# Two normalised copies of the residual stream exchange their buffers, and one is split ahead of the other

## The chip, the cores and the metric

The kernel runs on one core of one Trainium2 chip. The metric is the device time of one execution in microseconds (us); lower is better. Four engines matter here: TensorE (PE, matrix products into PSUM), VectorE (DVE), ScalarE (ACT), and SyncE (SP), whose queue issues most of the loads. Each engine works through its own list of instructions, and engines wait for one another by semaphores.

## The reference

The reference is a two-layer decoder trunk over 512 tokens of width 1024 in float32, held here with features on the 128 partitions, so that the stream `x` is eight tiles `x[0]` to `x[7]` of 128 x 512. Layer 0 mixes with a gated DeltaNet, layer 1 with sliding-window attention whose keys and values come from the stream as it stands after layer 0; each layer also attends to 256 memory tokens and ends with a SwiGLU network. What bears on this change is this:

```
x = x + swiglu(rms_norm(x, ln_ffn[layer]), w_gate_up[layer], w_down[layer])
if layer == N_A_LAYERS - 1:
    kv = rms_norm(x, ln_kv) @ w_kv          # keys and values of layer 1
...
h = rms_norm(x, ln_mix[layer])              # next layer
proj = h @ swa_w_q[bl]                      # its queries, and the memory queries
```

So once layer 0 is done, the same `x` is normalised twice with two gains: with `ln_mix[1]` for the queries, and with `ln_kv` for keys and values.

## The kernel before

**Arithmetic.** Products are made in a reduced form of float32. Each operand is split into a high and a low part, `hi = round(g*x)` by a copy on ACT (line 138) and `lo = g*x - hi` on DVE (line 154 with a gain, line 151 without), and each product is three matmuls: `wh*ah`, `wh*al`, `wl*ah` (`mm3`, lines 196 to 202). In a trace the activations' parts are called `h` and `l`, those of a weight tile `whi` and `wlo`. The row's scale of the norm, `rstd`, is not applied to `x` but to each product afterwards, so a split needs the finished `x[k]` and a gain, and nothing else. `pair` (line 160) takes a high and a low tile of 128 x 512 from a pool.

**The pools.** Two pools hold such pairs, eight each: `apool` and `bpool`. A slot can be written again when its last reader has run. Around the end of layer 0 they are used so:

| data | pool before | read until |
|---|---|---|
| normalised input of layer 0's SwiGLU | `bpool` | the last gate and up columns of layer 0 |
| SwiGLU products of layer 0's last third, six pairs (`whole`, line 1182) | `apool` | the last row of layer 0's down projection |
| layer 1's input with `ln_mix[1]` (list `h` of `swa`) | `apool` | the last of the queries |
| layer 1's input with `ln_kv` (list `hk`) | `bpool` | keys and values |
| outputs of layer 1's attentions (`beside`, line 1587) | `bpool` | layer 1's output projection |
| normalised input of layer 1's SwiGLU (`output`) | `apool` | layer 1's gate and up columns |
| products of layer 1's SwiGLU (`ffn8`) | `bpool` | its down projection |

**The stages around the change.** Layer 0's SwiGLU ends with eight rows of its down projection (lines 1273 to 1282). Each row `m` is 18 matmuls over the six pairs of products; then DVE scales the product (`fu<-pj,rstd`), adds it to `x[m]` (`x<-fu,x`), and ACT squares `x[m]` for the next norm's sum (`sq`, summed on DVE as `sqa`). The next stage is `swa` (line 1526). It fetches two memory tiles, splits `h` (line 1535), and begins the queries: tile 7 and tile 6 are the memory queries. `queries(6)` runs its 24 matmuls over `h[0]` to `h[7]`, then two steps (6 matmuls) of `queries(7)`, and then forms `rstd` of the new stream (`rstd_from`, line 1454): the summed squares are split (`rs`), multiplied by ones in two matmuls (`pt<-rs,ones`), and turned into `rstd` by a Ln and an Exp on ACT; DVE multiplies the rotary tables by it (`cosT`, `sinT`) and scales the product of tile 6 (`q<-pj,rstd`). In the text `hk` is split after `queries(6)` (line 1616). Then follow the rest of `queries(7)`, `score(6)` (`qk<-mk,q`), the keys (the first reader of `hk`), the values, `score(7)`, and the six pairs of windowed heads, whose queries, scores, softmax and output rows are interleaved.

**What sets the order.** The tile library lays out each engine's list when the program is built: it takes instructions that are ready by its own reckoning, the earlier in the program text the sooner, and an instruction whose slot is not free by that reckoning is passed over for one that can go. `nosync(a, b)` (line 114) adds an edge that places `a` behind `b` in that layout and costs no wait on the chip. Loads of weights are issued on SP's queue when one of the two `wraw` buffers comes free.

Of the kernel before, what the change touches and what calls it, by code (L numbers as in the profile page):

```python
# [39 lines left out]
G_MIX, G_FFN, G_KV, G_FIN = (0, 8), (16, 24), 32, 40  # L40
# [44 lines left out]
class Builder:  # L85
# [25 lines left out]
    def bank(self, tag, shape=(P, T)):  # L111
        return self.t(self.pp, list(shape), F32, tag, self.pbufs[tag])
# [131 lines left out]
    def build(self):  # L244
        tc, nc, a = self.tc, self.nc, self.a
        with ExitStack() as st:
            opened = lambda name, **kw: tc.tile_pool(name=name, bufs=1, reuse_waits="tile", **kw)
            pool = lambda name, **kw: st.enter_context(opened(name, **kw))
            cp = pool("const")
            self.wpool, self.apool = pool("w"), pool("acta")  # L250
            self.dpool = pool("scratch", space=DRAM)
            self.load_constants(cp)
            self.weng = nc.vector
            with opened("layer0", side="right") as self.mpool:
                with self.banks(pj=3, g=2, sc=3):
                    with opened("early", side="right") as ep:
                        self.mem_and_norm(ep)
                    with opened("gdn", side="right") as gp:
                        mix = self.gdn(gp)
                    self.bpool, xp = pool("actb"), pool("x")  # L260
                    self.x = [self.t(xp, [P, T], F32, f"x{k}") for k in range(KD)]
                    for k in range(KD):
                        nc.sync.dma_start(self.x[k], a["xT"][:, k, :])
                    self.rstd, self.cosT, self.sinT = (self.t(xp, [P, T], F32, n) for n in ("rstd", "cosT", "sinT"))
                    h = self.output(xp, 0, mix)
            with opened("ffn0", side="right") as fp, self.banks(pj=2, g=6):
                self.ffn8(fp, xp, 0, h, self.apool, rope=True)
            with self.banks(pj=2, qk=2, pt=2), opened("swa", side="right") as sp:
                h = self.output(xp, 1, *self.swa(sp))
            with opened("ffn1", side="right") as fp, self.banks(pj=2, g=6):  # L270
                self.ffn8(fp, xp, 1, h, self.bpool)

    def load_constants(self, cp):
        nc, a = self.nc, self.a
# [791 lines left out]
    def output(self, xp, layer, mix, begun=()):  # L1066

        nc, a = self.nc, self.a
        self.weng = nc.vector
        h = []  # L1070
        self.acc = None
        hpool = self.apool if layer else self.bpool
        bank = lambda m: self.bank(("pj", "pj", "pt")[m % 3] if begun else "g" if m % 4 == 3 else "pj")
        n, ws, lows = len(begun), [], []

        def early(m):
            if begun and n <= m < KD:
                ws.append(self.weight(a["wout"][layer, m]))
                lows.append(self.low)

        done = [list(row)[-1] for row in begun]
        for i in range(2):
            early(n + i)
        for m in range(KD):
            ps = done[m] if m < n else list(
                self.row(layer, m, mix, lambda: bank(m), ws.pop(0) if ws else None))[-1]
            self.ended = self.tt(nc.vector, self.x[m], ps, self.x[m], ALU.add)
            if m >= n - 1:
                early(m + 3)
            hl = self.pair(hpool)  # L1090
            self.split_gain(self.x[m], self.gain(G_FFN[layer], m), *hl)
            if m == 0 and lows:
                self.nosync(self.low, lows[-1])
            h.append(hl)
            self.acc = self.accumulate(xp, self.acc, self.x[m], m)
        self.behind = self.loaded if layer else None
        return h
# [428 lines left out]
    def swa(self, sp):  # L1526
        nc, a = self.nc, self.a
        memK, memV = self.fetch(sp, "mk"), self.fetch(sp, "mv")
        hk, h, qs, mix = [], [], {}, {}
        def normed(t, base, pool):  # L1530
            for k in range(KD):
                t.append(self.pair(pool))
                self.split_gain(self.x[k], self.gain(base, k), *t[k])

        normed(h, G_MIX[1], self.apool)
        sinks = self.small[:, 12:24].rearrange("p (b t) -> p t b", b=2)
        kk, vv = [], []

        def behind(step):

            return self.scalings[step - 1] if step > 0 else None

        def queries(t):
            w = self.weight(a["wq"][t], after=behind(t - 2) if t < 6 else None)
            ps = self.bank("pj")
            for k in range(KD):
                self.mm3(ps, w, k, h[k], k == 0, k == KD - 1)
                yield
            if t == 6:
                list(zip(range(2), beside7))  # L1550
                self.rstd_from(self.acc, *(self.t(sp, [P, T], F32R, "rs", 2) for _ in range(2)), after=self.last)
                for table in (self.cosT, self.sinT):
                    self.tt(nc.vector, table, table, self.rstd, ALU.mult)
            qs[t] = self.t(sp, [P, T], F32, "q", 3)
            if t < 6:
                self.rope(sp, ps, qs[t])
            else:
                self.tt(nc.vector, qs[t], ps, self.rstd, ALU.mult)
# [25 lines left out]

        def beside(t, *works):

            out = self.pair(self.bpool)
            steps = self.weighed(sp, got[t], *((vv, t) if t < 6 else (memV, t - 6)), out, t < 6)
            for work in works:
                list(work)  # L1590
                next(steps, None)
            mix[t] = out
            return self.ready, out
# [9 lines left out]
        def half():  # L1603
            if not free:
# [6 lines left out]
                         after=lambda m=m: behind(min(m + 4, 7)), **(own if m > 2 else {})) for m in range(5)]  # L1611
        some = lambda work, n: (next(work) for _ in range(n))
        got = {}
        beside7 = queries(7)
        list(queries(6))
        normed(hk, G_KV, self.bpool)
        list(beside7)
        score(6)
        keys()
# [7 lines left out]
        for t in range(6):  # L1627
            score(t)
            work, n = (queries(t + 2), (2, 3, 4)) if t < 4 else (rows[t - 4], (1, 1, 2))
            o = beside((6, 7, 0, 1, 2, 3)[t], *(some(work, i) if i < 4 else work for i in n))  # L1630
            softmax((7, 0, 1, 2, 3, 4)[t])
            settle(*o)
        o = beside(4, some(rows[0], 2), some(rows[1], 2), some(rows[2], 3))
        softmax(5)
        settle(*o)
        for m, n in ((2, 3), (3, 4)):
            list(some(rows[m], n))
        settle(*beside(5, some(rows[3], 2), some(rows[4], 3), (next(rows[m]) for m in (4, 4, 4, 0, 1))))
        for m in range(2, 5):
            list(some(rows[m], 1))  # L1640
# [110 lines left out]
```

## Time and profile before

| | |
|---|---|
| median of 3 runs | 1113.31 us (1112.72 to 1115.05) |
| time of the profiled execution | 1112.83 us |
| its span, first to last instruction | 1111.1 us |
| mean granted TensorE clock | 0.998 |
| busy: PE, PE weight loads, DVE, ACT | 99%, 90%, 84%, 63% of the span |

A row of the timeline gives the start, the time, the engine, the line, the operation, what it writes and reads, the shape, and how many instructions are merged into the row; brackets give idle time ahead of it and what ended it. Successive matmuls overlap in the trace, and so the distance from one start to the next tells how fast PE goes through them, not the duration of one. Layer 0's down rows stand from about 593 to 627 us from the start of the span, the start of `swa` from 627 us on.

### The profile page before, as it was taken

To read this page: it belongs to the slowest core of one execution; us is meant where nothing else is said; L and a number is where in the kernel's file an instruction comes from. 1 tells how busy PE (TensorE), PEld (TensorE's weight loads), DVE (VectorE), ACT (ScalarE), POOL (GpSimd) and SP (SyncE) were. 2 spreads that over 40 slices of the span, in tenths; PEclk is the share of its full clock that TensorE was granted. 3 is DMA by queue.
4 is the path that set the end of the run, shared out by engine and by line. 5 is a ranking of instruction groups with operands and counts; after the bars stand their busy time and mean duration, and the time that the engine had idled before them with its cause. 6 is when DMAs were issued, how large, how long until landed. Compare 5 with 4: busy or idle time off the path is not lost.

```text
span 1111.1 us, 21262 instructions
## 1 busy us (share of the span) xinstructions
PE 1100.6 (99%) x7957; PEld 998.9 (90%) x7957; DVE 937.0 (84%) x1890; ACT 697.2 (63%) x1470; POOL 105.9 (10%) x129
## 2 busy tenths in 40 slices
PE   9999999999999999999999999999999999999997
PEld 8888778877899999999998777788899999999996
DVE  7685977667899999999997977839999999998964
ACT  7588674466566656665565654866667466655644
POOL 0000000000011121112110000000111111121101
PEclk9999999999999999999999999999999999999999
DMA  8244352234567787778753321114677776778632
GB/s 320 98 151 142 114 142 82 90 98 145 150 173 183 189 190 191 179 184 199 191 147 99 117 74 40 58 58 142 159 176 192 189 195 184 186 198 203 148 86 90
DMA packets 81146, 165.36 MB, mean 149 GB/s; under 512 B 18588, under 2 KB 20148, under 8 KB 81044
## 3 DMA queue, kind: packets, MB, share of 16 engines
q1 hardware_dynamic: 64436, 133.87, 38.0%
q0 software_dynamic: 16320, 29.89, 16.5%
q8 instruction: 62, 1.02, 0.4%
q14 instruction: 40, 0.33, 0.1%
q10 hardware_dynamic: 288, 0.26, 0.1%
HBM read 156.98 MB, written 7.01 MB: 148 GB/s over the span
## 4 chain that ended last, share of the span: by engine, by line
PE 92%; DVE 5%; ACT 1%; issue 1%; DMA 0%; SPq 0%; DVEq 0%; ACTq 0%
PE g L144 54%; PE pj L144 26%; PE sc L144 6%; PE qk L144 3%; PE pt L144 2%; PE pt L148 1%; DVE wlo L151 1%; PE g L148 1%; DVE l L154 1%; DVE big L151 1%; DVE x L151 1%; DMA early<-in_early 0%; DVE fu L151 0%; DVE qv L154 0%; DVE btmp L151 0%
## 5 line engine op out<-in xcount | busy, mean ns | idle before, releaser
L138 ACT ACTIVATE whi<-wraw 128x512 fp32r<-128x512 f32 (+2 forms) x357 | 250.6, 711 | 161.4 <-PE g L144 66.3
L151 DVE TENSOR_TENSOR wlo<-wraw,whi 128x512 fp32r<-128x512 f32 (+2 forms) x357 | 280.5, 793 | 36.8 <-ACT whi L138 31.8
L144 PE MATMUL g<-T,whi 128*128 128x256 f32 x1280 | 228.3, 279 | 0.0
L144 PE MATMUL g<-h,wlo 128*128 128x256 f32 (+1 forms) x780 | 222.7, 285 | 0.6 <-DVE wlo L151 0.6
L144 PE MATMUL g<-l,whi 128*128 128x256 f32 (+1 forms) x780 | 222.6, 285 | 0.0
L144 PE MATMUL g<-h,whi 128*128 128x256 f32 (+1 forms) x780 | 222.4, 285 | 0.0
L144 PEld LDWEIGHTS g<-T,whi 128*128 128x128 f32 x1280 | 194.9, 188 | 0.5 <-DVE fu L154 0.5
L144 PE MATMUL pj<-h,whi 128*128 128x512 f32 (+1 forms) x460 | 182.0, 398 | 0.0
L144 PE MATMUL pj<-l,whi 128*128 128x512 f32 (+1 forms) x460 | 180.4, 393 | 0.4 <-DVE l L154 0.3
L144 PE MATMUL pj<-h,wlo 128*128 128x512 f32 (+1 forms) x460 | 179.8, 391 | 0.0
L144 PE MATMUL g<-T,wlo 128*128 128x256 f32 x640 | 178.5, 279 | 0.0
L144 PEld LDWEIGHTS g<-h,wlo 128*128 128x128 f32 x780 | 146.6, 188 | 2.8 <-DVE wlo L151 1.1
L144 PEld LDWEIGHTS g<-l,whi 128*128 128x128 f32 x780 | 146.6, 188 | 1.9
L144 PEld LDWEIGHTS g<-h,whi 128*128 128x128 f32 x780 | 146.6, 188 | 1.8
L144 PEld LDWEIGHTS g<-T,wlo 128*128 128x128 f32 x640 | 120.3, 188 | 0.0
L144 PEld LDWEIGHTS pj<-h,whi 128*128 128x128 f32 x460 | 86.4, 188 | 20.7 <-issue 4.1
L144 PEld LDWEIGHTS pj<-h,wlo 128*128 128x128 f32 x460 | 86.5, 188 | 18.0 <-issue 0.9
L144 PEld LDWEIGHTS pj<-l,whi 128*128 128x128 f32 x460 | 86.5, 188 | 17.8 <-DVE l L154 1.2
L138 ACT ACTIVATE whi<-ws 128x512 fp32r<-128x512 f32 x112 | 70.1, 626 | 38.9 <-PE g L144 36.8
L151 DVE TENSOR_TENSOR wlo<-ws,whi 128x512 fp32r<-128x512 f32 x112 | 77.1, 689 | 2.9 <-ACT whi L138 2.9
L1394 POOL DMA_DIRECT2D ws<-in_wgu x40 | 35.1, 878 | 414.6 <-DVE l L154 203.9
L138 ACT ACTIVATE fs<-g 128x256 f32<-128x256 f32 x168 | 61.5, 366 | 1.1 <-PE g L144 0.7
(398 smaller groups left out, 1929.6 us busy)
## 6 DMA issues: line engine op xcount, KB each, us to landing
wraw<-in_wgu SPq DMA_DIRECT2D x48, 512.0 KB, 4.0
ws<-in_wgu SPq DMA_DIRECT2D x80, 256.0 KB, 3.6
ws<-in_wgu POOLq DMA_DIRECT2D x80, 256.0 KB, 4.9
wraw<-in_win SPq DMA_DIRECT2D x26, 512.0 KB, 4.0
wraw<-in_wgu SPq DMA_DIRECT2D x40, 256.0 KB, 5.4
wraw<-in_wout SPq DMA_DIRECT2D x16, 512.0 KB, 3.4
ws<-in_wdn SPq DMA_DIRECT2D x32, 256.0 KB, 5.7
wraw<-in_wdn SPq DMA_DIRECT2D x16, 512.0 KB, 3.8
```

What stands on the lines that cost most here:

```text
L138: self.copied = self.nc.scalar.activation(out, in_, AF.Copy, **kw).ins
L144: return self.nc.tensor.matmul(out, lhsT, rhs, start=start, stop=stop, skip_group_check=more).ins
L148: return self.nc.tensor.transpose(out, in_, self.ident[:k, :k]).ins
L151: return eng.tensor_tensor(out=out, in0=a, in1=b, op=op).ins
L154: return self.nc.vector.scalar_tensor_tensor(out=out, in0=in0, scalar=scalar, in1=in1, op0=op0, op1=op1).ins
L1394: nc.gpsimd.dma_start(s1, a22, accum_op=ALU.add)
```

## The change

`h` and `hk` exchange their pools, and everything in layer 1 that follows in their slots exchanges with them, so that each pool still holds eight pairs at most: `h` goes into `bpool` and after it the normalised input of layer 1's SwiGLU; `hk` goes into `apool`, after it the attentions' outputs and the products of layer 1's SwiGLU. With that, `output` takes its pairs from `bpool` in both layers. New besides: `normed` can take two instructions as `after`, and each split of `hk` (its copy on ACT and its subtraction on DVE) is ordered behind the last split of `h` on the same engine by `nosync`. No instruction is added or removed.

```diff
@@ build
-                self.ffn8(fp, xp, 1, h, self.bpool)
+                self.ffn8(fp, xp, 1, h, self.apool)
@@ output
-        hpool = self.apool if layer else self.bpool
...
-            hl = self.pair(hpool)
+            hl = self.pair(self.bpool)
@@ swa
-        def normed(t, base, pool):
+        def normed(t, base, pool, after=()):
             for k in range(KD):
                 t.append(self.pair(pool))
                 self.split_gain(self.x[k], self.gain(base, k), *t[k])
-
-        normed(h, G_MIX[1], self.apool)
+                for ins, other in zip((self.copied, self.low), after):
+                    self.nosync(ins, other)
+
+        normed(h, G_MIX[1], self.bpool)
+        made = self.copied, self.low
@@ beside
-            out = self.pair(self.bpool)
+            out = self.pair(self.apool)
@@ swa, after queries(6)
-        normed(hk, G_KV, self.bpool)
+        normed(hk, G_KV, self.apool, made)
```

## The prediction

> **What bounds the kernel now.** I read the page first: the busy shares (of a span of 1111.1 us), and the engines on the chain that ended last.
>
> ```profile
> PE 1100.6 (99%) x7957; PEld 998.9 (90%) x7957; DVE 937.0 (84%) x1890; ACT 697.2 (63%) x1470; POOL 105.9 (10%) x129
> PE 92%; DVE 5%; ACT 1%; issue 1%; DMA 0%; SPq 0%; DVEq 0%; ACTq 0%
> ```
>
> PE carries 92% of the chain, so the change is worth what it alters in PE's waiting. The edit changes no instruction, only when the two sets of splits run; the place to look is therefore the seam from layer 0's last down row to the first queries. Next I read PE's timeline there and counted starts.
>
> ```profile
> 622.96 0.39 PE L144 MATMUL pj<-h,whi 128*128 128x512 f32 x1
> ...
> 627.04 0.39 PE L144 MATMUL pj<-h,whi 128*128 128x512 f32 x1
> ...
> 630.44 0.39 PE L144 MATMUL pj<-h,whi 128*128 128x512 f32 x1
> 630.92 0.50 PE L144 MATMUL pj<-l,whi 128*128 128x512 f32 x1
> ...
> 632.19 0.39 PE L144 MATMUL pj<-h,whi 128*128 128x512 f32 x1
> 632.85 0.50 PE L144 MATMUL pj<-l,whi 128*128 128x512 f32 x1 [0.27 <-DVE l L154]
> ...
> 634.81 0.62 PE L144 MATMUL pt<-rs,ones 128*128 128x512 f32 x2
> ...
> 639.49 2.00 PE L144 MATMUL qk<-mk,q 64*128 64x256 f32 x16
> 641.41 0.50 PE L144 MATMUL pj<-h,whi 128*128 128x512 f32 x1
> ```
>
> The last down row is the 18 matmuls from 622.96 to 627.04, so undisturbed PE takes 4.08/18 = 0.227 us for each. From 627.04 the 24 matmuls of queries(6) and 6 of queries(7) run until the sum of squares at 634.81: 7.77 us for 30, where 30 x 0.227 = 6.80 would do. **0.97 us is lost**, visibly at two starts that come 0.48 and 0.66 us after the one before: the low parts of h[5] (630.92) and of h[7] (632.85). The second bracket names the releaser: DVE's line 154. Then I read what DVE and ACT did there.
>
> ```profile
> 628.86 0.75 DVE L154 SCALAR_TENSOR_TENSOR l<-x,gains,h 128x512 fp32r<-128x512 f32 x1
> 629.52 0.69 DVE L151 TENSOR_TENSOR x<-fu,x 128x512 f32<-128x512 f32 x1
> 630.12 1.41 DVE L154 SCALAR_TENSOR_TENSOR l<-x,gains,h 128x512 fp32r<-128x512 f32 x2
> 631.44 0.69 DVE L151 TENSOR_TENSOR sqa<-sqa,sq 128x512 f32<-128x512 f32 x1
> 632.04 1.42 DVE L154 SCALAR_TENSOR_TENSOR l<-x,gains,h 128x512 fp32r<-128x512 f32 x2
> 633.37 0.69 DVE L151 TENSOR_TENSOR rs<-sqa,rs 128x512 fp32r<-128x512 f32 x1
> 633.97 0.75 DVE L154 SCALAR_TENSOR_TENSOR l<-x,gains,h 128x512 fp32r<-128x512 f32 x1
> 634.63 2.37 DVE L151 TENSOR_TENSOR wlo<-wraw,whi 128x1024 fp32r<-128x1024 f32 x2
> 636.92 0.69 DVE L151 TENSOR_TENSOR cosT<-cosT,rstd 128x512 f32<-128x512 f32 x1
> ...
> 638.13 0.69 DVE L151 TENSOR_TENSOR q<-pj,rstd 128x512 f32<-128x512 f32 x1
> ```
>
> ```profile
> 624.15 2.56 ACT L138 ACTIVATE h<-x,gains 128x512 fp32r<-128x512 f32 x4
> ...
> 630.84 1.32 ACT L138 ACTIVATE h<-x,gains 128x512 fp32r<-128x512 f32 x2
> 632.17 0.63 ACT L138 ACTIVATE rs<-sqa 128x512 fp32r<-128x512 f32 x1
> 633.39 1.06 ACT L138 ACTIVATE whi<-wraw 128x1024 fp32r<-128x1024 f32 x1 [0.59 <-PE pj L144]
> 635.47 0.69 ACT L132 ACTIVATE rstd<-pt,eps 128x512 f32<-128x512 f32 x1 [1.01 <-PE pt L144]
> 636.19 0.63 ACT L132 ACTIVATE rstd<-rstd 128x512 f32<-128x512 f32 x1
> ```
>
> ```profile
> L154 DVE SCALAR_TENSOR_TENSOR l<-x,gains,h x8: 743/751/753, 602.2 to 623.3; 128x512 fp32r<-128x512 f32 x8
> L154 DVE SCALAR_TENSOR_TENSOR l<-x,gains,h x16: 743/751/755, 602.2 to 634.0; 128x512 fp32r<-128x512 f32 x16
> ```
>
> The first two rows of ACT and DVE say why. Of the sixteen low parts eight were made by 623.3, the other eight stand from there to 634.0. `bpool` was free during the down rows, `apool` held the six pairs of products that these rows read, and so I read the early eight as h[0], h[1] (two free slots) and hk[0] to hk[5]. The four copies in one run at 624.15 start 1.2 us into the last down row, as its matmuls let go of slots: those are h[2] to h[5]. DVE then has eight `l`, two row ends and the chain of the sum in 624 to 634, and h[5] and h[7] come late.
>
> **The change part by part.**
>
> *h in `bpool`.* Its slots are free long before, so each h[k] can be split when x[k] is done, in the place where hk[0] to hk[5] stood. The last is h[7]. Before, x[7] was added at 629.52, behind an `l` of 0.66 us (628.86 to 629.52) that is now long done, so x[7] can start at about 628.9 and end at 629.5. The square and the copy on ACT take some 0.65 us each (2.56/4 in the run at 624.15), so the high part is there at 630.8 and the low part (0.66, half of 630.12 to 631.44) at 631.5. PE wants it with its 23rd matmul, 627.04 + 22 x 0.227 = 632.0. That covers the wait with 0.5 us to spare: **minus 0.97 us**. From below, the saving could be nothing, if PE's loss were something else than these waits; from above it cannot exceed the 0.97, since PE then runs at the pace of the down row. I take all of it, because both late starts fall on low parts of h and one names line 154.
>
> The trace offers a second reading of the same loss. The only idle time in brackets is 0.27 us, against 0.97 from the starts. [...] By the bracket alone the saving would be 0.27 and the time 1113.0; I go by starts.
>
> *hk behind h.* Eight copies (0.65 each) and eight low parts (0.66 each, 5.3 us on DVE) now follow h[7], from 631.5 on. On DVE there are 16 `l` as before, but ten of them after 623.3 where there were eight: 1.3 us more in a stretch without idle time. Behind them in the same lists stand:
>
> - The sum's low part `rs`. Squares, `sqa` and the copy make it ready at 631.5, it takes 0.6, and PE wants it 30 matmuls after 627.04, at 633.84. Slack 1.7 us, so two `l` of hk may pass it. Before, one did (the second of 632.04, then `rs` at 633.37, then the last). Cost nothing; cover 1.7 us.
> - `rstd`, then the tables and `q`. Before, from PE's 634.81 to the end of q, 638.13 + 0.69, were 4.01 us, and PE came to use q at 639.49: slack 0.67. New is that a copy of hk may be running on ACT when the Ln could start (up to 0.65) and an `l` on DVE ahead of `cosT` (up to 0.66). Together 1.31 less 0.67: from 0 to 0.6 us lost. Both being at their full length is unlikely: I take 0.1.
> - The keys' weights. The keys would start at 641.41 - 0.97 = 640.44 and want the low part of their weights with the third matmul, 640.9. Before, it was made in the first half of 634.63 to 636.92, 5 us early. Now DVE has from 631.5: 5.3 for hk, 0.6 for `rs`, 1.8 for `cosT`, `sinT` and q, 1.15 for the weight: to 640.35 if it never idles and the weight comes last. The cover is 0.55 us. If DVE idles 0.5 us for `rstd` and one of the reductions of the scores (0.6) is let past, 0.6 us are lost; if the weight is taken while h[7] waits for its copy, nothing. I take 0.1.
>
> hk[7] itself is read 21 matmuls after 640.44, 4.8 us later: covered.
>
> *SP's queue.* The load of the next query weights waits for a `wraw` buffer, and so for the low part of the keys' weights.
>
> ```profile
> 635.92 31.06 SPq L177 DMA_DIRECT2D wraw<-in_wq  x6
> ```
>
> ```profile
> wraw<-in_wq SPq DMA_DIRECT2D x8, 512.0 KB, 3.2
> ```
>
> It can move from 635.9 to 640.4. The load lands 3.2 us after its issue, copy (1.06) and low part (1.15) take 2.2, so the weight is ready at 645.8; PE first runs the 48 matmuls of keys and values, 640.44 + 10.9 = 651.3. Cover 5.5 us, cost nothing.
>
> *The slots after that.* Attention outputs, the SwiGLU's input and its products exchange pools with their predecessors and have the same readers in the same order, eight slots in both pools: nothing moves, unless the layout of the lists does.
>
> **Sum**: 0.97 - 0.1 - 0.1 = 0.77 us saved, against the profiled execution's 1112.83: 1112.06. The median shown is 0.48 above that execution, so **1112.5 us**.
>
> **The rivals.**
>
> *Given back.* Both small costs at their upper ends: 0.97 - 0.6 - 0.6, 1113.5. For it speaks that DVE is full from 628.86 to 638.8; against it, that ready work is taken in the order of the text, where q and the tables stand ahead of hk. If hk's splits were kept early by the layout and h late, there would be no change either, 1113.3; the new edge excludes that.
>
> *hk ahead of the sum: slower.* The lists are fixed ahead of the run. If the layout puts all eight `l` of hk ahead of `rs`, that ends at 631.5 + 5.3 + 0.6 = 637.4 against the 633.84 at which PE wants it, 3.5 us late; less 0.97, 2.6 us slower, **1115.9**. It decides from the fifth `l` on: 1.7 slack and 0.97 gained are four times 0.66. Against it: one was let past before, and `rs` is in the text ahead of hk. [...]
>
> *Another layout of layer 1.* The order of ready work decides later lists as well. In the windowed heads a weight's copy stands right behind the scaling of a softmax:
>
> ```profile
> 710.70 1.71 ACT L138 ACTIVATE sm<-sm,den 128x256 f32<-128x256 f32 x4 [0.56 <-DVE den L983]
> 712.31 1.05 ACT L138 ACTIVATE whi<-wraw 128x1024 fp32r<-128x1024 f32 x1
> ```
>
> Ahead of it, it would cost up to 1.05 us in each of six steps, 6.3 in all; an order better by as much in two or three steps would gain 2 to 3. Priced at 2.5 either way: 1110.0 or 1115.0, and up to 1119 at the far end. For it speaks that many edges in the code are there to hold such orders; against it, that those edges stay.
>
> **How the numbers follow.** The forecast 0.60 (its own range 1111.6 to 1113.4, with half a microsecond for the spread of the runs), given back or nothing 0.17, hk ahead of the sum 0.08, another layout 0.15, half to each side. 0.2%, about what a measurement of this kernel can tell, is 2.2 us: faster means under 1111.1, slower above 1115.5. Under it lie the better half of the layouts and a little of the forecast's spread, 0.12; above it hk ahead of the sum and most of the worse layouts, 0.13; between, 0.75. The range leaves out hk ahead of the sum and the far ends of the layouts: 1110.6 to 1115.2.
>
> **What would show it.** Right: sixteen `l` of which the first eight are all of h and the rest follow x[7]; no start of queries(6) more than 0.3 us after the one before, and the sum's `pt<-rs,ones` at 6.8 us after its first matmul instead of 7.8; qk and the keys' first matmul 0.8 to 1 us earlier than 639.49 and 641.41. Wrong: a new gap ahead of `pt<-rs,ones` (hk ahead of the sum), ahead of qk (`rstd`), or at the third matmul of the keys (the weight); or list orders after 660 us that differ.

## The result, and the profile after

The change makes the kernel slower: 1115.74 us (median of 11 runs, 1114.55 to 1118.88) beside 1112.74 us for the kernel before (11 runs, 1111.98 to 1115.05). The ratio is 1.0026, 95% interval 1.0018 to 1.0034: a loss of 2.9 us, clear of noise, where 1112.5 us had been forecast. The time lies above the forecast range of 1110.6 to 1115.2. That the loss is over 0.2%, and not just at it, the interval leaves open. The profiled execution took 1115.46 us, its span is 1113.6 us.

The page of the changed kernel, busy times and then the engines of the chain that ended last:

```profile
PE 1102.3 (99%) x7957; PEld 1001.8 (90%) x7957; DVE 937.4 (84%) x1890; ACT 697.5 (63%) x1470; POOL 105.9 (10%) x129
PE 94%; DVE 4%; issue 1%; ACT 1%; DVEq 0%; ACTq 0%
```

The counts of instructions are those of before, and the busy times of DVE and ACT differ by 0.4 us at most: only places have changed. The waits of PE show one that was not there (what waited, for whom, us in total, times, longest):

```profile
PE qk L144 <- DVE q L151: 2.2, 1, 2.2
```

PE's timeline at the seam gives it a place:

```profile
627.97 0.39 PE L144 MATMUL pj<-h,whi 128*128 128x512 f32 x1
...
632.73 0.39 PE L144 MATMUL pj<-h,whi 128*128 128x512 f32 x1
633.21 0.50 PE L144 MATMUL pj<-l,whi 128*128 128x512 f32 x1
...
635.17 0.62 PE L144 MATMUL pt<-rs,ones 128*128 128x512 f32 x2
...
642.16 2.00 PE L144 MATMUL qk<-mk,q 64*128 64x256 f32 x16 [2.25 <-DVE q L151]
644.09 0.50 PE L144 MATMUL pj<-h,whi 128*128 128x512 f32 x1
...
655.19 0.92 PE L144 MATMUL qk<-mk,q 64*128 64x256 f32 x6
```

The first query matmul is at 627.97, 0.93 later than before, while PE's list is the same and no new wait stands ahead of it. That much comes from stretches of slower pace earlier in this execution (last section). So lengths count here, not times of the clock:

| from, to | before | after |
|---|---|---|
| first query matmul to the sum `pt<-rs,ones` | 7.77 us | 7.20 us |
| the sum to the first `qk` of score(6) | 4.68 us | 6.99 us |
| that `qk` to the keys' first matmul | 1.92 us | 1.93 us |
| the keys' first matmul to score(7) | 11.15 us | 11.10 us |
| all four | 25.52 us | 27.22 us |
| score(7) to the end | 458.5 us | 458.5 us |

The seam gains 0.57 us where 0.97 was expected, and then loses 2.31 us ahead of score(6): 1.7 us more in all. The lists of ACT and then of DVE say where the 2.31 come from.

```profile
631.38 1.32 ACT L138 ACTIVATE h<-x,gains 128x512 fp32r<-128x512 f32 x2
632.61 0.61 ACT L138 ACTIVATE rs<-sqa 128x512 fp32r<-128x512 f32 x1
633.13 4.39 ACT L138 ACTIVATE h<-x,gains 128x512 fp32r<-128x512 f32 x7
637.43 0.67 ACT L132 ACTIVATE rstd<-pt,eps 128x512 f32<-128x512 f32 x1
638.00 1.04 ACT L138 ACTIVATE whi<-wraw 128x1024 fp32r<-128x1024 f32 x1
638.95 0.61 ACT L132 ACTIVATE rstd<-rstd 128x512 f32<-128x512 f32 x1
```

```profile
630.07 0.68 DVE L151 TENSOR_TENSOR x<-fu,x 128x512 f32<-128x512 f32 x1
630.67 1.22 DVE L151 TENSOR_TENSOR wlo<-wraw,whi 128x1024 fp32r<-128x1024 f32 x1
631.81 0.69 DVE L151 TENSOR_TENSOR sqa<-sqa,sq 128x512 f32<-128x512 f32 x1
632.41 1.41 DVE L154 SCALAR_TENSOR_TENSOR l<-x,gains,h 128x512 fp32r<-128x512 f32 x2
633.73 0.68 DVE L151 TENSOR_TENSOR rs<-sqa,rs 128x512 fp32r<-128x512 f32 x1
634.34 4.72 DVE L154 SCALAR_TENSOR_TENSOR l<-x,gains,h 128x512 fp32r<-128x512 f32 x7
639.08 1.23 DVE L151 TENSOR_TENSOR wlo<-wraw,whi 128x1024 fp32r<-128x1024 f32 x1
640.22 0.68 DVE L151 TENSOR_TENSOR cosT<-cosT,rstd 128x512 f32<-128x512 f32 x1
...
641.42 1.28 DVE L151 TENSOR_TENSOR q<-pj,rstd 128x512 f32<-128x512 f32 x2
```

Seven copies of `hk` stand in one run on ACT ahead of the Ln, and behind the Ln, ahead of the Exp, the copy of the values' weights. On DVE seven low parts of `hk` and the values' weights stand ahead of `cosT`. Against the rows of before the Ln starts 2.26 us after the sum instead of 0.66 (+1.60), the Exp 1.52 after the Ln instead of 0.72 (+0.80), `cosT` 1.27 after the Exp instead of 0.73 (+0.54). `q` follows `cosT` by 1.20 in both, and 0.62 us of slack that `q` had ahead of `qk` is used up: 1.60 + 0.80 + 0.54 - 0.01 - 0.62 = 2.31.

The seam accounts for 1.7 us of the 2.9. The rest doesn't show in this profile's seam; further runs and profiles of the same kernel show what makes most of it.

### The profile page after: what moved, and what is told of

Read it like the earlier page. It is cut to its first block, busy times and chain, and to the rows that moved or that the text cites. A ratio compares the mean times of both kernels' runs of the same rounds, so it can differ in the third digit from the quotient of the medians.

```text
span 1113.6 us, 21263 instructions
## 1 busy us (share of the span) xinstructions
PE 1102.3 (99%) x7957; PEld 1001.8 (90%) x7957; DVE 937.4 (84%) x1890; ACT 697.5 (63%) x1470; POOL 105.9 (10%) x129
## 4 chain that ended last, share of the span: by engine, by line
PE 94%; DVE 4%; issue 1%; ACT 1%; DVEq 0%; ACTq 0%
PE g L144 55%; PE pj L144 27%; PE sc L144 6%; PE qk L144 3%; PE pt L144 2%; PE pt L148 1%; DVE wlo L151 1%; PE g L148 1%; DVE l L154 1%; DVE qv L154 0%; DVE x L151 0%; DVE fu L151 0%; DVE big L151 0%; ACT h L138 0%; DVE btmp L151 0%
```

## The experiments

Theory **lists**: the places in ACT's and DVE's lists make the loss, and the pools have no part in it. Rival **pools**: the exchange itself costs. A second theory, **clock**, came up with the first runs: the new wait also lowers TensorE's clock. The "sum" is the pair of matmuls `pt<-rs,ones`; "the sum to `qk`" is the distance from there to the first matmul of score(6). Each ratio is against the kernel before, timed beside it on the same chip.

### Each half alone

The exchange without the edges:

```diff
-        normed(hk, G_KV, self.apool, made)
+        normed(hk, G_KV, self.apool)
```

> The pools exchanged, without the order edges: the lists of all engines are those of before, but h[2] to h[5] and hk[2] to hk[5] have changed places. If the order edges cost (lists), no loss: h[5] no longer stalls PE, but h[7] still stands behind two low parts of hk, so PE reaches the sum of squares at the same time as before; 0.0 us, at best -0.4, ratio 0.9996 to 1.0002, qk 4.7 us after the sum. If the exchange of pools costs, +1.7 to +3, ratio 1.0016 to 1.0027.

1112.91 us, ratio 1.0000 (0.9991 to 1.0008). First query matmul to the sum 7.76 us, the sum to `qk` 4.68, all four stretches 25.51: the seam of before to 0.01 us. The stall at h[5] is gone, and h[7]'s low part comes as late as ever (PE's timeline):

```profile
632.96 0.50 PE L144 MATMUL pj<-l,whi 128*128 128x512 f32 x1 [0.64 <-DVE l L154]
```

Here the first of two waits on one chain of late work was removed, and it moved into the second: 0.64 us at h[7], where it was 0.27 before. The new pools alone are neutral.

The edges without the exchange, `h` and `hk` in the pools of before (against the kernel before, in part):

```diff
-        def normed(t, base, pool):
+        def normed(t, base, pool, after=()):
...
+                for ins, other in zip((self.copied, self.low), after):
+                    self.nosync(ins, other)
...
-        normed(hk, G_KV, self.bpool)
+        normed(hk, G_KV, self.bpool, made)
```

> The pools of before, with the order edges alone: every split of hk behind the last split of h. If the edges cost (lists): seven low parts of hk and one weight stand ahead of the tables' scaling, qk comes 7.0 us after the sum of squares instead of 4.7; no gain from h, since its slots are as late as before: +2.2 us, ratio 1.0020. If the exchange of pools costs and the edges do not: 0, ratio 1.0000.

1114.44 us, ratio 1.0016 (1.0007 to 1.0025); the sum to `qk` 6.87 us. DVE's and PE's timelines:

```profile
632.88 4.72 DVE L154 SCALAR_TENSOR_TENSOR l<-x,gains,h 128x512 fp32r<-128x512 f32 x7
637.52 1.22 DVE L151 TENSOR_TENSOR wlo<-wraw,whi 128x1024 fp32r<-128x1024 f32 x1
```

```profile
626.64 0.39 PE L144 MATMUL pj<-h,whi 128*128 128x512 f32 x1
...
633.72 0.63 PE L144 MATMUL pt<-rs,ones 128*128 128x512 f32 x2
...
640.59 2.91 PE L144 MATMUL qk<-mk,q 64*128 64x256 f32 x16 [2.13 <-DVE q L151]
```

The same run of seven and nearly the same wait: the edges make the loss, and the pools don't. The expectation that nothing would be gained at the sum missed, and that says as much about the change as the loss does. The sum comes 633.72 - 626.64 = 7.08 us after the first query matmul, 0.69 earlier than before, though `h` stays in the pool with the late slots:

| | first query matmul to the sum | the sum to `qk` |
|---|---|---|
| before | 7.77 us | 4.68 us |
| new pools alone | 7.76 us | 4.68 us |
| edges alone | 7.08 us | 6.87 us |
| both (the change) | 7.20 us | 6.99 us |

So the edges make the gain too. What held PE up at the sum were low parts of `hk` ahead of those of `h` on DVE, and not the late slots by themselves. New is also that the 16 `qk` take 2.91 us instead of 2.00. To that the section on the clock returns.

### hk behind rstd and q

The exchange, with `hk`'s splits ordered behind the Exp of `rstd` on ACT (`self.rooted`) and behind the `q` of tile 6 on DVE (`self.asked`), in part:

```diff
-        normed(hk, G_KV, self.apool, made)
+        normed(hk, G_KV, self.apool, (self.rooted, self.asked))
```

> The changed kernel with the edges moved: each split of hk stands behind the Exp that makes rstd (ACT) and behind the product q of tile 6 (DVE), instead of behind the last split of h. If the lists cost: qk again 4.7 us after the sum of squares, the sum 7.2 us after the first matmul of queries(6) as in the changed kernel, so -0.6 us against before, ratio 0.9995; the keys are not held, because hk's low parts follow each other at 0.67 us and PE uses one in 0.68. If the exchange of pools costs: still +1.7 to +3, ratio 1.0016 to 1.0027. If hk now comes too late for the keys, a wait at the keys' matmuls on line 154, up to 2 us.

1113.07 us, ratio 1.0001 (0.9992 to 1.0010). The sum to `qk` is 4.68 us again, so the 2.31 us do hang on what stands ahead of `rstd` and `q`. 0.59 us are gained at the sum; what becomes of them, DVE's and PE's timelines show:

```profile
637.38 0.68 DVE L151 TENSOR_TENSOR q<-pj,rstd 128x512 f32<-128x512 f32 x1
637.98 5.38 DVE L154 SCALAR_TENSOR_TENSOR l<-x,gains,h 128x512 fp32r<-128x512 f32 x8
```

```profile
654.25 0.66 PE L148 MATMUL pt<-consts,rs 128*128 128x128 f32 x4 [0.45 <-DVE rs L151]
```

Eight low parts now stand ahead of the score's maxima, DVE is late for the rest of the stretch, and PE waits 0.45 us at the transposes of the values. Compared start by start with before, PE is 0.75 us ahead at 633 (0.17 of it since before the seam), 0.24 at the transposes and 0.09 at 666: given back.

### The weights between, and a share of the splits

The changed kernel with the values' weights split behind the Exp (ACT, `self.rooted`) and behind the `q` of tile 6 (DVE, `self.asked`), the lines that set the order:

```diff
-            ps = self.project(a["wkv"][1], hk)
+            w = self.weight(a["wkv"][1], after=(self.rooted, self.asked))
+            ps = self.project(None, hk, w=w)
```

> The changed kernel with one more pair of edges: the split of the values' weights is put behind the Exp of rstd on ScalarE and behind the q of tile 6 on VectorE. It takes out the 0.80 us that the weight's copy stands between Ln and Exp and the 0.54 us that its low part comes after them on VectorE. Theory lists: from the sum to the first score matmul 6.99 - 0.80 - 0.54 = 5.65 us (4.68 before), an idle stretch of TensorE of 0.9 to 1.0 us, too short for the half clock in any run: 0.97 slower there less 0.57 gained at the sum, +0.4 us, ratio 1.0004. Rival, the seven copies and seven low parts of hk alone set the last q (they fill VectorE to 639.1 anyway): 6.4 to 6.99 us, and half clock in a part of the runs as before, ratio 1.0010 to 1.0020.

1113.59 us, ratio 1.0005 (0.9996 to 1.0014). The sum to `qk` is 5.74 us; PE's wait is

```profile
638.98 2.00 PE L144 MATMUL qk<-mk,q 64*128 64x256 f32 x16 [1.00 <-DVE q L151]
```

The weight's share was forecast as 0.80 + 0.54 = 1.34 us and is 6.99 - 5.74 = 1.25. With the weight out of the way the seven splits cost the other 1.06. So more than half of the loss hangs on an instruction that the change doesn't name: before, this weight's copy ran on ACT at 633.39, well ahead of the Ln; now the copies of `hk` stand in that place, and it was laid between Ln and Exp.

The same, with `hk[0]` to `hk[3]` free, and the keys' weights behind the last split of `h` (against the changed kernel, in part):

```diff
-                for ins, other in zip((self.copied, self.low), after):
+                for ins, other in zip((self.copied, self.low), after if k > 3 else ()):
...
-            self.rope(sp, self.project(a["wkv"][0], hk), kk[0])
+            w = self.weight(a["wkv"][0], after=made)
+            self.rope(sp, self.project(None, hk, w=w), kk[0])
```

> The changed kernel with the edges shared out otherwise: hk[0] to hk[3] free, hk[4] to hk[7] behind the last split of h, the keys' weights behind it too, and the values' weights behind the Exp of rstd and the q of tile 6. Theory lists: h[5] and h[7] are no longer late (first query matmul to the sum 6.8 us instead of 7.8) and at most two or three splits of hk stand ahead of rstd and q (sum to scores 4.7 us as before): 0.9 us faster, ratio 0.9992. Rival given back: what is gained at the sum is lost again by 666 us, as TensorE waits for VectorE at the transposes of the values, where VectorE has the same work and no idle time: 1.0000. Rival lists again: four splits are still too many ahead of q, sum to scores 5.3 to 6 us: 1.0000 to 1.0004.

1113.02 us, ratio 0.9999 (0.9990 to 1.0008). The sum to `qk` is 4.68 us, as expected. But the sum comes 7.28 us after the first query matmul and not 6.8, and of the 0.49 us gained 0.38 are given back at the transposes. DVE's timeline:

```profile
641.69 1.23 DVE L151 TENSOR_TENSOR wlo<-wraw,whi 128x1024 fp32r<-128x1024 f32 x1 [0.58 <-ACT whi L138]
642.84 0.68 DVE L947 TENSOR_REDUCE mx<-qk 128x2 f32<-128x512 f32 x1
```

The next query weights' low part waits for a copy whose load came late (ACT idles 2.28 us for it, to 640.60). The keys' weights, now split behind the last of `h`, are done with their `wraw` buffer only at 637.4 (their low part starts at 636.17 and takes 1.23 us), where it was 635.9 before, and the copy starts 3.2 us after that. The first maximum of score(6), behind that low part, starts 3.15 us after that score's first matmul, where it was 2.11 before (641.60 - 639.49). The softmax is 1.0 us late from there, and the values' product, behind the softmax on DVE, too (PE's timeline):

```profile
655.16 0.66 PE L148 MATMUL pt<-consts,rs 128*128 128x128 f32 x4 [0.41 <-DVE rs L151]
```

With three more kinds of edge on DVE for these two places and for h[7] (two low parts of `hk` behind `x[7]`, the query weights behind the maxima, the next ones behind the values' product), in part:

```diff
+                if after and k in (2, 3):
+                    self.nosync(self.low, self.summed)
...
+            if t in (0, 1):
+                self.nosync(self.low, self.topped6 if t == 0 else self.valued1)
```

> The kernel with four_late's edges and three more on VectorE: the low parts of hk[2] and hk[3] behind the sum into x[7]; the low part of the first query weights behind the last maximum of score(6) instead of ahead of the first; the low part of the second query weights behind the values' product with rstd. Theory: in four_late VectorE stood ahead of PE twice, at h[7]'s low part (two low parts of hk ahead of x[7], 1.3 us) and at the values' product (1.2 us of weight ahead of it, and a softmax begun 1.0 us later behind a weight). With both cleared: first query matmul to the sum 6.8 us (7.28 in four_late, 7.77 before), sum to scores 4.7, no wait ahead of the transposes of the values: 0.9 us faster than before, ratio 0.9992. Rival, given back once more: VectorE and ScalarE have as much to do by 666 us as before and the first windowed scores wait for the query's rotation or the softmax: 1.0000.

1113.23 us, ratio 0.9999 (0.9990 to 1.0007). The four stretches are 25.04 us, 0.48 less than before, and nothing is given back (458.5 us from score(7) to the end). A gain of 0.48 in 1113 is below what these runs can tell: no version here was measurably faster than before. Why it is 0.48 and not 0.97, DVE's and PE's timelines say:

```profile
629.55 0.69 DVE L151 TENSOR_TENSOR x<-fu,x 128x512 f32<-128x512 f32 x1
630.15 1.41 DVE L154 SCALAR_TENSOR_TENSOR l<-x,gains,h 128x512 fp32r<-128x512 f32 x2
631.48 0.68 DVE L151 TENSOR_TENSOR sqa<-sqa,sq 128x512 f32<-128x512 f32 x1
632.08 1.41 DVE L154 SCALAR_TENSOR_TENSOR l<-x,gains,h 128x512 fp32r<-128x512 f32 x2
```

```profile
632.88 0.50 PE L144 MATMUL pj<-l,whi 128*128 128x512 f32 x1 [0.19 <-DVE l L154]
```

Between `x[7]` and h[7]'s low part DVE still does 1.3 us of other low parts and the sum of squares. Work of that length filled the place in the other versions too (in the changed kernel the keys' weights, 630.67). In `four_late` the place was empty, DVE idled 0.76 us there, but two low parts of `hk` stood ahead of `x[7]` and made that late instead. That without any such work the whole 0.97 would come was not tried.

### The clock

The changed kernel again, beside the first three experiments:

> The changed kernel once more, unaltered. If the loss lies in the seam alone (from the end of layer 0's last down row to the keys' first matmul: 14.37 us before, 16.12 after, 1.75 more), the seam is again 16.1 us and the time 1.7 us above before, ratio 1.0016. If something outside the seam adds the rest of the measured 3.0 us, the profile shows it again in the same place (layer 0 ran 0.9 us later between 400 and 600 us in the first profile) and the ratio is 1.0027.

1115.94 us, ratio 1.0018 (1.0009 to 1.0027). Its profile has the same stretches, 7.18 and 6.99 us, but from `qk` to the keys' first matmul 3.45 us instead of 1.93. The windows view (stretch; its length; busy time and instructions of PE, PEld, DVE, ACT and POOL; granted TensorE clock; DMA share; GB/s):

```profile
637.76:641.17 3.41, 1.42 (x7) 0.84 (x5) 3.39 (x5) 2.16 (x3) 0.00 (x0) 1.00 0.17 36
641.17:644.58 3.41, 3.13 (x14) 2.55 (x16) 2.82 (x5) 0.01 (x1) 0.00 (x0) 0.50 0.45 149
```

The clock is halved for 3.41 us behind the wait, which costs 1.5 us more. In the first profile it was 1.00 throughout the seam. The edges of these stretches are the records' own: the entries of granted clock in the two traces read

```
after        1.0 from   6.68 us for 1102.505 us, then 0.5
after_again  1.0 from   6.29 us for  634.879 us, 0.5 for 3.413 us, 1.0 for 467.626 us, then 0.5
```

and 634.879 is 186 times 3.4133, 1102.505 is 323 times: the clock changes on a grid of 3.413 us. The wait ahead of score(6) is 2.28 us in this profile and 2.25 us in the first, both shorter than one step of the grid, and half clock followed here and not there. So theory **clock** says that part of a window idle is enough, and that what counts is how much of the wait falls into one. Two kernels test it, and the changed one is run three times more.

First, TensorE kept at work: 8 matmuls that nobody reads between the end of queries(7) and score(6):

```diff
+        ps, last = self.bank("pt"), self.last
+        for i in range(8):
+            self.nosync(self.mm(ps, self.ones_r, h[i][0], i == 0, i == 7), last)
         score(6)
```

> The changed kernel with 8 more matmuls (ones times the high parts of h, 8 x 0.23 = 1.8 us) put on TensorE between the end of queries(7) and score(6), where TensorE idles 2.25 us for the last q; nobody reads their result, and the lists of VectorE and ScalarE stay as they are. Theory lists + clock: the last q still comes at 642.1 (sum to first score matmul 6.99 us, 4.68 before), but the idle stretch is cut to about 0.4 us, so no half clock follows in any run: scores 1.93 us long, 1.7 us slower than before in every run, ratio 1.0015, mean clock of the runs 0.998 or 0.999 as in before. Theory lists alone (the low clock in the records is a chip's own disturbance and not caused by the gap): the same ratio and the same mix of mean clocks as the changed kernel beside it, 1.0020 to 1.0026.

1114.76 us, ratio 1.0015 (1.0006 to 1.0024).

```profile
641.27 0.92 PE L144 MATMUL qk<-mk,q 64*128 64x256 f32 x6 [0.39 <-DVE q L151]
```

The idle stretch is 0.39 us, `q` is as late as before that edit (7.00 us from the sum to `qk`), the four stretches are 27.22 us, and all 11 runs have a mean clock of 0.998 or 0.999. This is the loss of the lists alone, 1.7 us.

> The changed kernel once more, beside the three others. Theory lists + clock: 1.7 us slower than before where the mean clock is 0.998 or 0.999, some 1.5 us more in the runs where it is 0.996 or 0.997, which are most: ratio 1.0020 to 1.0026. Theory lists alone: 1.0015 with no second group.

1116.59 us, ratio 1.0024 (1.0015 to 1.0034), beside `warm` on one chip; its profile has full clock, with this window of the grid holding most of the wait:

```profile
639.28:642.69 3.41, 1.48 (x14) 1.35 (x16) 3.41 (x6) 0.55 (x1) 0.00 (x0) 1.00 0.47 154
642.69:646.10 3.41, 3.41 (x19) 2.56 (x16) 2.45 (x7) 1.43 (x6) 0.00 (x0) 1.00 0.48 156
```

The ratio is the expected one, but not by the expected cause: only one of its 9 runs has a mean clock under 0.998, while 6 of the 9 lie between 1116.1 and 1116.8. Here the low clock doesn't explain the distance to `warm`; a slower pace that the clock records don't show may (last section). That stays open. It also means that `warm`, with no low clock in 11 runs beside one in 9, doesn't show by itself that the added matmuls kept the clock up.

Second, the wait made longer: three products on DVE ahead of the tables and of `q` (in part; an edge puts that `q` behind them too):

```diff
+                spare = self.t(sp, [P, T], F32, "rs", 2)
+                for i in range(3):
+                    late = self.tt(nc.vector, spare, self.rstd, self.rstd, ALU.mult)
                 for table in (self.cosT, self.sinT):
-                    self.tt(nc.vector, table, table, self.rstd, ALU.mult)
+                    self.nosync(self.tt(nc.vector, table, table, self.rstd, ALU.mult), late)
```

> The changed kernel with three more products of rstd with itself on VectorE (0.60 us each, written to a spare buffer that nobody reads) ahead of cosT, sinT and the q of tile 6. TensorE's wait ahead of score(6) grows by 1.8 us, from 2.25 to about 4.05 us. Theory clock on a grid: the records change the clock at multiples of 3.41 us from the first rise, and a window with more than about 1.95 us idle (1.99 and 2.13 in the two profiles that had the half clock, 1.64 and 1.93 in the two that had not) is followed by one at half clock; 4.05 us put over 2 us into one window wherever it falls, so the half clock comes in every run: mean clock 0.996 or 0.997 (0.998 at most) in all, against about half of the runs of the changed kernel. Time: 1.8 us and some 0.7 us more than the changed kernel's, 4 to 5.5 us slower than before, ratio 1.0036 to 1.0050. Theory lists alone: the added 1.8 us and no other clock: ratio 1.0031 to 1.0036, mean clock 0.998 or 0.999 in about as many runs as the changed kernel.

1119.38 us, ratio 1.0057 (1.0043 to 1.0071), mean clock 0.995 to 0.997 in all 5 runs: the low clock comes every time, as expected. The size was forecast too small. The wait is 4.33 us, and two windows follow at half clock, not one:

```profile
638.22:641.63 3.41, 1.28 (x6) 0.74 (x4) 3.32 (x5) 2.01 (x3) 0.00 (x0) 1.00 0.15 37
641.63:645.04 3.41, 1.21 (x6) 1.04 (x8) 3.41 (x6) 0.00 (x0) 0.00 (x0) 0.50 0.31 117
645.04:648.46 3.42, 3.42 (x16) 2.32 (x13) 2.13 (x5) 1.02 (x4) 0.00 (x0) 0.50 0.48 156
```

By the theory that is what has to come: the first window holds 2.13 us of idle time and halves the second, the second holds 2.20 and halves the third.

Two more profiles of the changed kernel:

> The changed kernel, for one more profile of the seam. Theory clock on a grid: half clock ahead of or in the scores if the idle time of TensorE inside one 3.41-us window of the records' grid is over about 1.95 us, and full clock if it is under that; sum to scores 6.99 us either way.

> The same once more, for a second profile: half clock if over about 1.95 us of the wait ahead of score(6) lie inside one window of 3.41 us, full clock if less; sum to scores 6.99 us either way.

The first, 1116.18 us, has full clock, the second, 1119.32 us, half clock for one window from 642.33. Here are the windows of the grid that hold most of the wait ahead of score(6), with PE's busy time in the window and the clock granted in the next, and in the row of `values_late` a window of another kind, where PE runs out of work at the end of the program:

| profile | window | PE busy of 3.41 us | clock of the next |
|---|---|---|---|
| long_gap, second | 641.63 to 645.04 | 1.21 | 0.50 |
| after_look2 | 638.92 to 642.33 | 1.25 | 0.50 |
| long_gap, first | 638.22 to 641.63 | 1.28 | 0.50 |
| order_only | 638.12 to 641.53 | 1.28 | 0.50 |
| after_again | 637.76 to 641.17 | 1.42 | 0.50 |
| values_late, its end | 1102.15 to 1105.57 | 1.47 | 0.50 |
| after_third | 639.28 to 642.69 | 1.48 | 1.00 |
| after | 638.15 to 641.56 | 1.77 | 1.00 |
| after_look1 | 636.38 to 639.79 | 2.18 | 1.00 |

The order is clean: 1.47 and less are followed by half clock, 1.48 and more are not. It holds beyond these rows. Laid over all fourteen profiles from their first full clock on, the grid has some 4500 windows; every one with 1.47 us or less is followed by half clock and no other is. The ends of the programs supply the rest of the low ones, such as 0.99 in the first profile of the changed kernel and 1.41 in `long_gap`.

Where the wait falls in the grid differs from one execution to the next: in the rows of the changed kernel alone PE is busy for 1.25 to 2.18 us of the window. Take a wait of 2.25 us and a bound at 3.41 - 1.47 = 1.94 us of idle time. If all phases were equally likely, (3.41 - 2.25 + 2 x (2.25 - 1.94))/3.41 = 52% of the executions should be hit. Of 33 runs of the changed kernel 17 have a mean clock of 0.996 or 0.997, while all 79 runs of the kernel before whose clock is on record have 0.998 or 0.999. But the sets are uneven: 8 of 11, 7 of 11, 1 of 9, 1 of 2. So the agreement with 52% is partly luck, and what sets the phase on a chip no run here tells. Within the first two sets the runs with the low clock have a median 1.5 and 1.8 us above the others (1116.2 against 1114.7, 1116.0 against 1114.1).

The lists' 1.7 us in every profile and 1.5 us more in about half of the runs make some 2.5 us; the three ratios of the changed kernel (1.0026, 1.0018, 1.0024) are 2.0 to 2.9 us. For the third of them, `after_third`, the sum is right and its second term isn't: the low clock is missing there.

## Why the prediction was wrong, point by point

**h in `bpool`: minus 0.97 us.** Right that both late starts were late low parts of `h`, and that starts tell more than the bracket's 0.27 us. Wrong in the cause: the prediction put the gain down to the free slots, but the new pools alone gain 0.01 us and the edges alone 0.69. The gain came from what the prediction held for a side condition, `hk` behind `h`. Too large in size as well: 0.57 in the changed kernel, and 0.48 to 0.69 in all versions with edges. The size failed at h[7]'s low part "at 631.5", 4.5 us behind the first query matmul: in `best` it ends 5.2 us behind it. The working left out that `sqa` stands ahead of it on DVE (0.6 us) and that ready work fills DVE while ACT squares and copies. Its "`l` of 0.66 us that is now long done" ahead of `x[7]` was also still there in the changed kernel, at 629.41.

**`rs`: slack of 1.7 us, cost nothing.** Right: two `l`, one of them h[7]'s, stand ahead of it, it starts at 633.73 and ends 0.8 us before the sum.

**`rstd`, then the tables and `q`: "from 0 to 0.6 us lost", taken at 0.1.** This is the step that failed: 2.31 us. It granted one copy of `hk` ahead of the Ln and one `l` ahead of `cosT`, as if the lists gave way to whatever is more urgent. They were laid out in advance, and put seven of each there, with a weight's copy between Ln and Exp and its low part behind the seven. `rstd_first` takes all of that away and `qk` comes 4.68 us after the sum; `values_late` takes the weight away and 1.25 us go. That weight, the values', had no term in the sum at all, though its low part is the second of the two `wlo` at 634.63 in the rows of before. The upper bound had to be worked out from what could stand there: seven copies of 0.62 us, 4.4 us on ACT.

**Keys' weights: 0 to 0.6 us.** None was lost at the keys. The low part was made early, at 630.67, ahead of h[7]'s, and so took its part of the first term instead.

**SP's queue: cost nothing.** Right for the change: the stretches behind are as long as before. In `four_late`, where the keys' weights kept a buffer 1.5 us longer, the late load did delay DVE: 0.58 us of idle time ahead of 641.69.

**The slots after that, and the layout of layer 1: nothing.** Right, 458.5 us behind score(7) in both; `swap_free` shows that the exchange costs 0.0.

**The rivals.** "hk ahead of the sum" had the right mechanism, eight splits in a fixed list ahead of something urgent, and nearly the right time (1115.9), but at the wrong place: `rs` was let through, the Ln and `q` weren't. That its time nearly came true is luck. It got a chance of 0.08 on the ground that `q` and the tables stand ahead of `hk` in the text; that did not hold, and it would seem because `hk` is ready sooner: its copies start at 633.13, while the Ln, 0.66 us behind the sum at best, could not before 635.8. And the Ln does not pass the copies that stand ahead of it: ready behind the sum at 635.8, it runs only at 637.43, as the last of them ends. "Given back" is what happens to `rstd_first` and `four_late`.

**What no part of the prediction had:** a wait of 2.25 us on TensorE that costs another 1.5 us by the clock, in 17 of 33 runs.

## What to carry to other kernels

Work that becomes ready earlier than the urgent chain can be laid ahead of it, even where the text has it behind; when a change makes a whole set of splits ready at once, price the chain behind it with the whole set ahead of it on each queue, then add an edge for what must not pass, and look once more at what fills the place. A stall with two late inputs is removed only with the later one (`swap_free` cleared one of two and gained 0.01 us). Where a change has two halves, run each alone before you believe why it gains: here the pools, which gave the change its name, did nothing, and the edges made both the gain and the loss. And a new wait of TensorE can cost more than its length: this one turned 1.7 us into 3.2 in about half of the runs.

## What the runs showed of the hardware

- The granted TensorE clock changes on a grid of 3.413 us, and a window with PE busy for 1.47 us or less was followed by one at 0.50, with 1.48 or more by one at 1.00, in all windows of the fourteen profiles. One window at half clock costs 1.5 to 1.6 us here: in `after_again` and `after_look2` the 16 `qk` take 3.45 and 3.55 us instead of 1.93. That the bound is one on PE's busy time in the window is inferred from this order.
- In some executions PE goes 0.9% slower for 80 to 200 us at a granted clock of 1.00. The windows view of 50 us (PE's busy time with its matmuls in brackets comes first behind the length), before and after_third:

```profile
900.00:950.00 50.00, 50.00 (x431) 50.00 (x430) 48.38 (x96) 33.35 (x67) 9.56 (x11) 1.00 0.74 187
```

```profile
900.00:950.00 50.00, 50.00 (x427) 50.00 (x426) 47.85 (x96) 33.55 (x67) 9.20 (x11) 1.00 0.75 186
```

  427 matmuls of the same shape where 431 fit, with a mean clock of 1.00 in both. In after_third this lasts from about 870 to 1070 us and makes 1.9 us; in the first profile of the changed kernel it lies ahead of the seam. It came with kernels that have no half clock too (`rstd_first`, `warm`, `swap_free`). Compared start by start with the profile before, such stretches lie only in three places of the program, at about 400 to 512, 514 to 594 and 866 to 1066 us: five, six and five of the fourteen profiles have them. They come and go from one execution of a kernel to the next and cost about 0.7, 0.8 and 1.9 us each. That is of the size of the spread between runs of one kernel; that they make it is not shown, since most runs have no profile. What causes them, and whether they come more often with one list than with another, no run here tells.
